# Twelve instead of eight weight pairs in the first pass of an MLP up-projection (Strassen-Winograd form, two-layer trunk)

## The chip, the cores and the metric

The kernel runs on one NeuronCore of a Trainium2 chip. The metric is the device time of one execution in microseconds. TensorE does the matrix products, VectorE (DVE) and ScalarE (ACT) prepare their operands and take their results, GpSimd (POOL) does small work and issues the stores of intermediate results, and SyncE (SP) issues the loads. Each of these engines works through its own list of instructions in order; the lists are written at build time by a scheduler that simulates the program, and semaphores tie them together.

## The reference

A trunk of two layers on a residual stream of 1024 tokens x 1024 features. Layer 0 mixes tokens with multi-head latent attention, layer 1 with a gated linear recurrence (HGRN2). Each is followed by a squared-ReLU MLP with 4096 inner features, and every sub-layer is wrapped in two RMS norms:

```python
def sq_relu_mlp(h, w1, w2):
    a = jax.nn.relu(h @ w1)
    return (a * a) @ w2
...
    h = h + rms_norm(m, norm_gains[layer, 1])        # m: the token mixer's output
    a = rms_norm(h, norm_gains[layer, 2])
    h = h + rms_norm(sq_relu_mlp(a, mlp_w1[layer], mlp_w2[layer]), norm_gains[layer, 3])
```

All inputs and the output are float32.

## The kernel before, in words

**Products.** Every float32 operand is split into a high part (fp32r, made by ACT) and a low part (the rest, made by DVE from the high part): `split`, lines 76 and 77. A product then takes three matmuls (`mm3`, lines 81 to 83): high x high, high x low, low x high. The second matmul of the three needs the moving operand's low part, the third the weights' low part.

**The stages.** Attention, its output projection with the first norm, MLP of layer 0, recurrence, MLP of layer 1. Each MLP has an up part (`mlp_up`, 1024 to 4096 features) and a down part (`mlp_down`). The change is in `mlp_up`.

**The up part.** It forms w1-transposed times activations by one level of the Strassen-Winograd scheme, with seven block products in place of eight. The activations are four blocks: B11 and B21 are the two feature halves of tokens 0 to 511, B12 (the tile `whole`, or in layer 1 `acc`) and B22 those of tokens 512 to 1023. Four sums of these blocks, T1 to T4, are made by DVE in steps of 128 x 1024 and split (`tsums12`, `tsums34`, lines 742 to 763). The 4096 inner features are taken in 16 *pairs* of 128-column blocks, p = 0 to 15. For each pair seven products of 12 matmuls of 512 columns are made: with B11, with B21 (on top of the first, in the same PSUM bank), with T2, T1, T3, B22 and T4.

**Two passes.** The products with B11 and B21 need tokens 0 to 511 alone. So for the first `EARLY` pairs they are made ahead, while the last tokens of the stage before are still on their way through the norms, and then the T sums; what they give (`sP1`, the product with B11, and `h11`, the first output block) is stored to DRAM and loaded again in the second pass (abridged):

```python
            for p in range(0, EARLY, 2):
                with tc.high_priority(offset=AHEAD[layer]):
                    for i in (p, p + 1):
                        w12[i] = w_parts(raw_early(i))
                        first[i], sP1 = first_two(i, w12[i][:, :, :4])
                        POOL.dma_start(psp[i * P:(i + 1) * P, :], sP1)
                    for i in (p, p + 1):
                        add_second(i, first[i], w12[i][:, :, 4:])
            tsums12()
...
            for p in range(NP):
                rA, rB = raw_half(p, 0), raw_half(p, 1)
                if p < EARLY:          # h11 and sP1 are loaded; w_parts(rB[:, :, P:])
                    others(p, rA, rB, ...)
                else:                  # first_two, w_parts of rA's half and of all of rB, add_second
                    ...
```

For an early pair the second pass is the five other products, 60 matmuls; for any other pair it is all seven, 84 matmuls. `others` (line 824) makes two weight sums for DVE to split: `s12` (lines 826, 827; for T2 and T1) and `s34` (lines 832, 833; for T3 and B22), adds the products up (lines 837, 844, 848, 851, 854), squares them on ACT (806, 807) and stores six results per pair (line 803).

**Buffers that matter here.** In the first pass `sP1` and `h11` go through two buffers `he`, which are free again when their stores have landed. The split weights `w` have five buffers. The raw weights have three buffers `raw` in the up part, of 512 KB each: a first-pass load (`raw_early`, line 785, one per pair) takes turns in two of them, a second-pass load (`raw_half`, line 791, two per pair) in all three. The first-pass products lie in two PSUM banks `mm`, the products with T2 in two banks `tr`.

**What sets the order.** The scheduler alone. The first pass has a priority of its own (`AHEAD`); the T sums and the second pass stand in program order behind it, and the scheduler merges them by its own estimate of when operands are ready.

Of the kernel before, what the change touches and what calls it, by code (L numbers as in the profile page):

```python
# [36 lines left out]
ROPE_BASE = 10000.0  # L37
LAG = (150, 100, 250)
AHEAD = (150, 150)
EARLY = 8  # L40
SCALE = (NOPE + ROPE) ** -0.5


# [15 lines left out]
def trunk(ctx, tc, x, x_t, positions, norm_gains, mla_w_in, mla_q_norm, mla_kv_norm, mla_w_uq, mla_w_ukv, mla_w_o,  # L59
# [9 lines left out]
    def new(p, shape, dt, tag, bufs=None):  # L69
        uid[0] += 1  # L70
        kw = {} if bufs is None else {"bufs": bufs}
        return p.tile(shape, dt, tag=tag, name=f"{tag}_{uid[0]}", **kw)
# [629 lines left out]
    hsp = new(dram, [7, NP * P, 512], F32, "hsp")  # L702
    psp = new(dram, [EARLY * P, 512], F32, "psp")

    def mlp_up(layer):
# [4 lines left out]
        with tc.tile_pool(name=f"up{layer}", bufs=1, side="left", reuse_waits="tile") as wp:  # L710
# [54 lines left out]
            def product(ps, w, X, more=False):  # L765

                for k in range(4):
                    mm3(ps, (w[:, 0, k], w[:, 1, k]), (X[:, 0, k], X[:, 1, k]), not more and k == 0, k == 3, more)
# [5 lines left out]
            def h512():  # L774
                tag = ring[hs["n"] % len(ring)]
                assert tag != "h2" or hs["more"]
                hs["n"] += 1
                p, bufs = {"he": (G, 2), "h": (wp, NH), "h2": (hs["more"], NM)}[tag]
                return new(p, [P, 512], F32, tag, bufs)
# [8 lines left out]
            def raw_half(p, kh):  # L788
                hs["r"] += 1
                r = new((wp, G0, G)[hs["r"] % 3], [P, 1024], F32, "raw").rearrange("p (k c) -> p k c", c=256)  # L790
                SP.dma_start(r, w1[:, kh * 4:(kh + 1) * 4, p * 256:(p + 1) * 256])
                return r
# [12 lines left out]
            def act2(h, src):  # L805
                ACT.activation(h, src, AF.Relu)
                ACT.activation(h, h, AF.Square)  # L807

            def first_two(p, wa):

                a = new(PG, [P, 512], F32, "mm")
                product(a, wa, B11)
                sP1 = h512() if p >= EARLY else new(G, [P, 512], F32, "he", 2)
                ACT.activation(sP1, a, AF.Copy)  # L814
                return a, sP1

            def add_second(p, a, w12):
                product(a, w12[:, :, :, :P], B21, True)
                h11 = h512() if p >= EARLY else new(G, [P, 512], F32, "he", 2)
                act2(h11, a)  # L820
# [50 lines left out]

            for p in range(0, EARLY, 2):

# [16 lines left out]
            for p in range(NP):  # L890
                rA, rB = raw_half(p, 0), raw_half(p, 1)
                if p < EARLY:
                    h11 = h512()
# [495 lines left out]
```

## Time and profile before

| | us |
|---|---|
| median of three runs | 2336.49 (2329.7 to 2338.51) |
| the profiled execution's own time | 2335.4 |
| its span, first to last instruction | 2333.7 |
| TensorE busy | 2266.3 (97%), 11487 matmuls |
| DVE busy | 1595.5 (68%) |
| ACT busy | 1170.1 (50%) |
| DMA | 333.12 MB, mean 143 GB/s |

The up part of layer 0 lies at about 480 to 806 us of the span, that of layer 1 at about 1693 to 2025 us. A matmul's record in this profile is longer than its step, because matmuls are pipelined: in a full stretch one of 512 columns starts every 0.227 us, while its record lasts 0.39 us. So a busy share near 100% is not a full TensorE; the count of matmuls in a stretch of fixed length, and the starts in the timeline, tell more. A stretch counts every instruction that touches it, those across its ends too.

### The profile page before, as it was taken

To read this page: it belongs to the slowest core of one execution; us is meant where nothing else is said; L and a number is where in the kernel's file an instruction comes from. 1 tells how busy PE (TensorE), PEld (TensorE's weight loads), DVE (VectorE), ACT (ScalarE), POOL (GpSimd) and SP (SyncE) were. 2 spreads that over 40 slices of the span, in tenths; PEclk is the share of its full clock that TensorE was granted. 3 is DMA by queue.
4 is the path that set the end of the run, shared out by engine and by line. 5 is a ranking of instruction groups with operands and counts; after the bars stand their busy time and mean duration, and the time that the engine had idled before them with its cause. 6 is when DMAs were issued, how large, how long until landed. Compare 5 with 4: busy or idle time off the path is not lost. (4 is left out here: it accounts for less than half of the span.)

```text
span 2333.7 us, 30701 instructions
## 1 busy us (share of the span) xinstructions
PE 2266.3 (97%) x11487; PEld 1912.8 (82%) x11487; DVE 1595.5 (68%) x2287; ACT 1170.1 (50%) x1893; POOL 346.1 (15%) x718
## 2 busy tenths in 40 slices
PE   8999999998999999999999999999989999999998
PEld 8789998876788888888888888888777888888886
DVE  5658886378766557588666667756678776566696
ACT  5436554364444444445565546755464444444443
POOL 1300000021222100001232213312121221100001
PEclk9999999999999999999999999999999999999999
DMA  7010002464654484565612334222355644663664
GB/s 221 23 33 10 10 10 71 145 231 161 219 171 162 167 288 144 180 215 177 207 47 90 101 98 136 79 76 73 95 186 191 222 155 149 222 238 114 223 214 158
DMA packets 229283, 333.12 MB, mean 143 GB/s; under 512 B 16743, under 2 KB 136590, under 8 KB 229134
## 3 DMA queue, kind: packets, MB, share of 16 engines
q1 hardware_dynamic: 205326, 251.45, 33.4%
q0 software_dynamic: 23808, 79.71, 9.3%
q8 instruction: 90, 1.47, 0.3%
q14 instruction: 59, 0.48, 0.1%
HBM read 247.22 MB, written 83.89 MB: 142 GB/s over the span
## 5 line engine op out<-in xcount | busy, mean ns | idle before, releaser
L77 DVE TENSOR_TENSOR w<-raw,w 128x1024 fp32r<-128x1024 f32 (+1 forms) x240 | 278.1, 1164 | 165.4 <-ACT w L76 164.6
L76 ACT ACTIVATE w<-raw 128x1024 fp32r<-128x1024 f32 (+1 forms) x240 | 237.8, 996 | 211.6 <-PE mm L83 82.4
L81 PE MATMUL mm<-A,w 128*128 128x512 f32 x832 | 329.6, 397 | 6.8 <-ACT he L814 2.9
L82 PE MATMUL mm<-A,w 128*128 128x512 f32 x832 | 327.4, 394 | 0.6 <-DVE A L77 0.6
L83 PE MATMUL mm<-A,w 128*128 128x512 f32 x832 | 325.7, 393 | 0.0
L76 ACT ACTIVATE w<-s 128x1024 fp32r<-128x1024 f32 x156 | 164.8, 1059 | 312.0 <-PE tr L83 120.5
L77 DVE TENSOR_TENSOR w<-s,w 128x1024 fp32r<-128x1024 f32 x156 | 190.2, 1221 | 140.8 <-ACT w L76 140.3
L81 PEld LDWEIGHTS mm<-A,w 128*128 128x128 f32 x832 | 157.5, 189 | 43.2 <-ACT he L814 4.0
L145 POOL TENSOR_TENSOR rstd<-rstd,nhalf 128x1 f32<-128x1 f32 x56 | 44.4, 794 | 965.5 <-DVE rstd L144 939.0
L83 PEld LDWEIGHTS mm<-A,w 128*128 128x128 f32 x832 | 157.3, 189 | 32.9
L82 PEld LDWEIGHTS mm<-A,w 128*128 128x128 f32 x832 | 157.4, 189 | 32.5 <-DVE A L77 1.0
L82 PE MATMUL mm<-w,w 128*128 128x512 f32 x432 | 168.6, 390 | 0.7 <-DVE w L77 0.7
L83 PE MATMUL mm<-w,w 128*128 128x512 f32 x432 | 168.3, 390 | 0.0
L81 PE MATMUL mm<-w,w 128*128 128x512 f32 x432 | 154.2, 391 | 0.8 <-DVE y L1036 0.4
L803 POOL DMA_DIRECT2D hsp<-h x176 | 94.8, 540 | 349.0 <-ACT h L807 176.8
L81 PE MATMUL mm<-w,A 128*128 128x256 f32 (+2 forms) x352 | 111.8, 320 | 4.3 <-ACT A L76 3.5
L83 PE MATMUL mm<-w,A 128*128 128x256 f32 (+2 forms) x352 | 111.3, 318 | 0.0
L82 PE MATMUL mm<-w,A 128*128 128x256 f32 (+2 forms) x352 | 110.6, 316 | 0.0
L83 PE MATMUL c<-T,w 128*128 128x512 f32 x256 | 99.4, 391 | 4.4 <-DVE w L77 4.4
L81 PE MATMUL c<-T,w 128*128 128x512 f32 x256 | 100.3, 392 | 1.6 <-ACT w L76 1.6
L82 PE MATMUL c<-T,w 128*128 128x512 f32 x256 | 99.7, 389 | 0.0
L81 PEld LDWEIGHTS mm<-w,w 128*128 128x128 f32 x432 | 81.0, 188 | 19.2 <-ACT u L1034 0.8
(441 smaller groups left out, 5648.4 us busy)
## 6 DMA issues: line engine op xcount, KB each, us to landing
raw<-in_mlp_w_dram SPq DMA_DIRECT2D x92, 512.0 KB, 5.0
hsp<-h POOLq DMA_DIRECT2D x176, 256.0 KB, 3.2
s<-in_mlp_w_dram SPq DMA_DIRECT2D x80, 512.0 KB, 5.9
raw<-hsp SPq DMA_DIRECT2D x76, 512.0 KB, 3.9
raw<-in_hgrn_w_in_dram SPq DMA_DIRECT2D x64, 512.0 KB, 4.2
sx<-hsp SPq DMA_DIRECT2D x36, 512.0 KB, 4.0
hsp<-he POOLq DMA_DIRECT2D x48, 256.0 KB, 3.3
xt<-in_x_dram SPq DMA_DIRECT2D x16, 512.0 KB, 6.1
```

Of the source, the lines that this page charges most:

```text
L76: ACT.activation(dst[:, 0], src, AF.Copy)
L77: DVE.tensor_tensor(dst[:, 1], src, dst[:, 0].bitcast(F32), ALU.subtract)
L81: PE.matmul(ps, lhs[0], rhs[0], start=start, stop=False, skip_group_check=more)
L82: PE.matmul(ps, lhs[0], rhs[1], start=False, stop=False, skip_group_check=more)
L83: PE.matmul(ps, lhs[1], rhs[0], start=False, stop=stop, skip_group_check=more)
L145: POOL.tensor_tensor(r, r, nhalf[:, :1], ALU.pow)
L803: POOL.dma_start(hsp[i, p * P:(p + 1) * P, :], h)
```

## The change

One constant grows: the first pass takes pairs 0 to 11, not 0 to 7. The scratch tensor `psp` follows it in size.

```diff
-EARLY = 8
+EARLY = 12
```

In each layer, pairs 8 to 11 thus get 24 matmuls ahead of the T sums' products instead of between their own other products. Each of them then has one load of 512 KB more (`raw_early`), one store more (`psp`, 256 KB) and two loads more (`h11` and `sP1`, 256 KB each). The matmuls are the same in number. The splits too are the same in their elements: in the first pass one of 1024 columns (the B11 and the B21 weights together), in the second one of 512 less by the first half and one of 512 instead of 1024.

How the scheduler's lists move is seen at three places, all in layer 0; layer 1 is alike but for details that the text names. In the names, `s` is a sum, `T_858`, `T_854`, `T_856`, `T_855` are T1, T2, T4 and T3, `whole` is B12, `A_748` to `A_750` are B11, B21 and B22; the last number of a name is a tile's own number.

**DVE, where the T sums begin.** Before:

```order
L745 TENSOR_TENSOR s_5376<-whole_4349,A_748_4343 128x1024
L77 TENSOR_TENSOR A_750_4345<-tr_5059,A_750_4345 128x4x128
L746 TENSOR_TENSOR s_5376<-s_5376,A_748_4343 128x1024
L747 TENSOR_TENSOR s_5377<-A_750_4345,s_5376 128x1024
L745 TENSOR_TENSOR s_5386<-whole_4349,A_748_4343 128x1024
L748 TENSOR_TENSOR s_5377<-s_5377,A_750_4345 128x1024
L77 TENSOR_TENSOR T_858_5079<-s_5376,T_858_5079 128x1024
L746 TENSOR_TENSOR s_5386<-s_5386,A_748_4343 128x1024
L77 TENSOR_TENSOR T_854_5075<-s_5377,T_854_5075 128x1024
L747 TENSOR_TENSOR s_5387<-A_750_4345,s_5386 128x1024
```

With the change:

```order
L745 TENSOR_TENSOR s_5524<-whole_4349,A_748_4343 128x1024
L77 TENSOR_TENSOR A_750_4345<-tr_5059,A_750_4345 128x4x128
L746 TENSOR_TENSOR s_5524<-s_5524,A_748_4343 128x1024
L747 TENSOR_TENSOR s_5525<-A_750_4345,s_5524 128x1024
L745 TENSOR_TENSOR s_5534<-whole_4349,A_748_4343 128x1024
L77 TENSOR_TENSOR T_858_5079<-s_5524,T_858_5079 128x1024
L748 TENSOR_TENSOR s_5525<-s_5525,A_750_4345 128x1024
L746 TENSOR_TENSOR s_5534<-s_5534,A_748_4343 128x1024
L77 TENSOR_TENSOR w_5399<-raw_5397,w_5399 128x1024
L77 TENSOR_TENSOR w_5452<-raw_5450,w_5452 128x1024
L747 TENSOR_TENSOR s_5535<-A_750_4345,s_5534 128x1024
```

The weight splits of pairs 9 and 10 (`w_5399`, `w_5452`) now stand among the T sums; that of pair 11 follows six rows later. From the row behind line 746's second to the end of pair 0's second weight split (`s34`) there are 27 rows with the change, 22 of them of 1024 columns and 5 of 512.

**DVE, where pair 1 begins its second pass.** Before, its sums (`s_5542`, `s_5548`) and the split of the first of them (`w_5545`) stand together:

```order
L77 TENSOR_TENSOR w_5453<-s_5435,w_5453 128x1024
L844 TENSOR_TENSOR h_5469<-mm_5456,h_5451 128x512
L826 TENSOR_TENSOR s_5542<-raw_5531,raw_5533 128x4x128
L77 TENSOR_TENSOR T_855_5076<-s_5426,T_855_5076 128x1024
L77 TENSOR_TENSOR w_5539<-raw_5533,w_5539 128x512
L832 TENSOR_TENSOR s_5548<-raw_5531 128x4x128
L827 TENSOR_TENSOR s_5542<-s_5542,raw_5531 128x4x128
L833 TENSOR_TENSOR s_5548<-raw_5533,s_5542 128x4x128
L848 TENSOR_TENSOR h_5484<-c_5471,h_5469 128x512
L77 TENSOR_TENSOR w_5545<-s_5542,w_5545 128x1024
```

With the change:

```order
L77 TENSOR_TENSOR T_855_5076<-s_5574,T_855_5076 128x1024
L77 TENSOR_TENSOR w_5601<-s_5583,w_5601 128x1024
L826 TENSOR_TENSOR s_5690<-raw_5679,raw_5681 128x4x128
L832 TENSOR_TENSOR s_5696<-raw_5679 128x4x128
L827 TENSOR_TENSOR s_5690<-s_5690,raw_5679 128x4x128
L833 TENSOR_TENSOR s_5696<-raw_5681,s_5690 128x4x128
L77 TENSOR_TENSOR w_5687<-raw_5681,w_5687 128x512
L826 TENSOR_TENSOR s_5803<-raw_5792,raw_5794 128x4x128
L832 TENSOR_TENSOR s_5809<-raw_5792 128x4x128
L827 TENSOR_TENSOR s_5803<-s_5803,raw_5792 128x4x128
L833 TENSOR_TENSOR s_5809<-raw_5794,s_5803 128x4x128
L77 TENSOR_TENSOR w_5693<-s_5690,w_5693 128x1024
```

The T sums are all done before pair 1 begins, and the four sums of pair 2 (`s_5803`, `s_5809`) now stand between pair 1's sums and the split `w_5693` of the first of them. In layer 1 the same four stand there.

**SP, the loads around the end of the first pass.** Before (line 785 is a first-pass load, 791 one half of a pair's second-pass weights, 894 and 896 the loads of `h11` and `sP1`):

```order
L785 DMA raw_5323<-in_mlp_w_dram 128x8x128
L791 DMA raw_5396<-in_mlp_w_dram 128x4x256
L791 DMA raw_5398<-in_mlp_w_dram 128x4x256
L791 DMA raw_5531<-in_mlp_w_dram 128x4x256
L894 DMA he_5400<-hsp_5068 128x512
L896 DMA he_5402<-psp_5069 128x512
L791 DMA raw_5533<-in_mlp_w_dram 128x4x256
```

With the change:

```order
L785 DMA raw_5450<-in_mlp_w_dram 128x8x128
L791 DMA raw_5679<-in_mlp_w_dram 128x4x256
L785 DMA raw_5471<-in_mlp_w_dram 128x8x128
L791 DMA raw_5544<-in_mlp_w_dram 128x4x256
L791 DMA raw_5546<-in_mlp_w_dram 128x4x256
L791 DMA raw_5681<-in_mlp_w_dram 128x4x256
L791 DMA raw_5792<-in_mlp_w_dram 128x4x256
L791 DMA raw_5794<-in_mlp_w_dram 128x4x256
L791 DMA raw_5905<-in_mlp_w_dram 128x4x256
L791 DMA raw_5907<-in_mlp_w_dram 128x4x256
L894 DMA he_5548<-hsp_5068 128x512
L896 DMA he_5550<-psp_5069 128x512
```

The weights of pairs 0 to 3 are now asked for ahead of pair 0's `h11` and `sP1`, where before three halves were. On TensorE, 60 matmuls (72 in layer 1) stand between the end of pair 7's first-pass products and the first matmul with T2, where before there were none; 76 stand ahead of the first that needs the low part of pair 0's first weight sum, 120 ahead of the first with T3, and 136 ahead of the first that needs the low part of pair 1's. The last three counts are the same in both layers. The lists of the recurrence between the two MLPs differ in places too, with the same instructions but for one load of an ACT function table fewer.

## The prediction, made before the changed kernel ran

> **What bounds the kernel now.** I read the page first, for the engine that is full; then the busy times by 100 us, for where that engine is not; then the same by 10 us, and the timelines of TensorE and DVE in the stretches found.
>
> ```profile
> span 2333.7 us, 30701 instructions
> PE 2266.3 (97%) x11487; PEld 1912.8 (82%) x11487; DVE 1595.5 (68%) x2287; ACT 1170.1 (50%) x1893; POOL 346.1 (15%) x718
> ...
> 500.00:600.00 100.00, 88.27 (x369) 69.88 (x368) 80.40 (x98) 48.72 (x73) 16.25 (x30) 0.95 0.52 177
> 600.00:700.00 100.00, 99.49 (x438) 81.64 (x437) 74.57 (x106) 47.49 (x69) 23.70 (x44) 1.00 0.59 195
> ...
> 1700.00:1800.00 100.00, 86.57 (x368) 68.96 (x367) 80.77 (x97) 50.23 (x77) 19.29 (x33) 0.95 0.52 173
> 1800.00:1900.00 100.00, 100.00 (x443) 82.81 (x442) 76.15 (x110) 46.51 (x68) 23.68 (x44) 1.00 0.63 213
> ```
>
> The columns of a stretch are its length, then busy time and instructions of TensorE, its weight loads, DVE, ACT and POOL, then the granted TensorE clock, the DMA share and GB/s. TensorE sets the time: a full 100 us hold 443 matmuls, one per 0.226 us. Two stretches hold 369 and 368, 149 matmuls or 34 us short together, and these lie where each MLP goes over from its first pass to its second. Nothing else the change touches has slack of this size.
>
> ```profile
> 533.40:560.80 27.40, 20.43 (x67) 15.09 (x67) 25.25 (x29) 13.02 (x17) 1.08 (x2) 0.81 0.37 122
> 1740.20:1766.10 25.90, 16.78 (x53) 12.38 (x53) 24.97 (x27) 9.88 (x11) 0.54 (x1) 0.80 0.33 108
> ...
> 533.17 0.39 PE L83 MATMUL mm<-A,w 128*128 128x512 f32 x1
> 535.19 0.50 PE L81 MATMUL tr<-T,w 128*128 128x512 f32 x1 [1.63 <-ACT w L76]
> 538.89 0.80 PE L83 MATMUL tr<-T,w 128*128 128x512 f32 x1 [2.49 <-DVE w L77]
> 541.19 0.63 PE L82 MATMUL tr<-T,w 128*128 128x512 f32 x1
> 541.62 0.63 PE L83 MATMUL tr<-T,w 128*128 128x512 f32 x1
> 549.78 0.50 PE L83 MATMUL c<-T,w 128*128 128x512 f32 x1 [2.18 <-DVE w L77]
> 560.58 0.39 PE L82 MATMUL c<-T,w 128*128 128x512 f32 x1
> 560.81 0.39 PE L83 MATMUL tr<-T,w 128*128 128x512 f32 x1
> ...
> 1740.01 0.39 PE L83 MATMUL mm<-A,w 128*128 128x512 f32 x1
> 1743.87 0.50 PE L81 MATMUL tr<-T,w 128*128 128x512 f32 x1 [3.48 <-ACT w L76]
> ```
>
> In layer 0 the first pass ends with the matmul at 533.17; the next could start at 533.40. TensorE then waits for splits of the weight sums of pair 0, which stand on DVE among the T sums, and DVE is busy 25.25 of 27.40 us. The matmul at 560.81 is the 67th of the stretch, so 66 are done before it. 66 x 0.227 us (the pace of starts in a full stretch, as from 560.58 to 560.81) = 15.0 us of work in 27.4: **12.4 us lost.** In layer 1, 52 matmuls (53 less the last) take 11.8 us of 25.9: **14.1 us lost.** A part of it is a lower clock: the starts 541.19 and 541.62 are 0.43 us apart.
>
> **The change part by part.** *Cover gained.* 96 matmuls per layer come ahead of this point, 21.8 us. What has to be ready, and when, follows from DVE's own steps:
>
> ```profile
> 525.06 1.22 DVE L746 TENSOR_TENSOR s<-s,A 128x1024 f32<-128x1024 f32 x1
> 526.20 1.22 DVE L77 TENSOR_TENSOR T<-s,T 128x1024 fp32r<-128x1024 f32 x1
> 544.43 0.68 DVE L832 TENSOR_TENSOR s<-raw 128x512 f32<-128x512 f32 x1
> 545.03 0.68 DVE L833 TENSOR_TENSOR s<-raw,s 128x512 f32<-128x512 f32 x1
> ...
> 1733.81 1.22 DVE L746 TENSOR_TENSOR s<-s,A 128x1024 f32<-128x1024 f32 x1
> ```
>
> A step of 1024 columns takes 1.135 us from start to start, one of 512 columns 0.60. Up to the second step of line 746, which ends at 526.2, the list has the same steps as before. Then come 27 to the end of pair 0's second weight split: 22 x 1.135 + 5 x 0.60 = 28.0, so 554.2. The raw weights of pair 0 may add 1.2 us: they wait for the slot of pair 11's first-pass weights, whose split ends 8 steps after 526.2, at 535.3, and a load takes 4.6 us:
>
> ```profile
> L791 SPq DMA_DIRECT2D raw<-in_mlp_w_dram x64: 367/368/577, 503.3 to 1967.1; - x64
> ...
>   DVE s L826: 32.2, 18
> ...
> DMA to landing us min/median/max: 3.7/4.6/8.5
> ```
>
> So all T sums and pair 0's weights are ready at 555.4. TensorE needs the last of them for T3, 120 matmuls after 533.4, at 560.6; the T2 product needs pair 0's first split 76 matmuls after, at 550.6, and that split is six steps from the end (four of 1024, two of 512), done at 549.7. In layer 0 nothing is late here. In layer 1 the same two are 1757.4 (1740.2 + 17.2) and 1758.3 (three and two steps before the 1762.9 of the next part): **0.9 us** of waiting. The four extra splits cost DVE nothing: pairs 8 to 11 have as many columns to split as before, and it lies under matmuls in both places. So the 12.4 and 14.1 us go: **26.5 us.**
>
> *What is late next.* DVE's list now has pair 2's four sums ahead of the split that pair 1's T2 product needs. They read raw weights, of which three buffers exist, and DVE waited for raw weights at line 826 eighteen times before, 32.2 us in all (row above). Step by step in layer 0: pair 0's buffer is read to the end by line 832, at 555.4 less 1.135 (the second split), 1.135 (the last T3 split) and 0.6 (line 833) = 552.5; pair 1's second half lands there 4.6 us later, 557.1; three sums of pair 1 free the third buffer at 558.9; pair 2's second half lands in it at 563.5; four sums, 565.9; then pair 1's split, **567.0**. TensorE needs it 136 matmuls after 533.4, at 564.2: **2.8 us** of waiting. Layer 1, the same from 1733.8 (here 28 steps follow a step earlier in the list, 23 x 1.135 + 5 x 0.60 = 29.1, with no wait for pair 0): 1762.9, buffer free at 1760.0, landed 1764.6, third buffer free 1766.4, landed 1771.0, split done **1774.5**, needed at 1740.2 + 0.9 + 30.8 = 1771.9: **2.6 us**, and 20 matmuls later **0.8 us** more, where line 844 of pair 0, which the B22 product waits for, stands behind pair 3's load (done 1779.8, needed 1779.0). Together 0.9 + 2.8 + 2.6 + 0.8 = **7.1 us back.** Bounds: with the shortest landing, 3.7 us, two loads in a row at each place save 1.8 us each, and 7.1 falls to 3.5; with the longest, 8.5 us, they add 7.8 us each, 15.6, and 7.1 grows to 22.7.
>
> *The clock.* A stall can cost more than itself.
>
> ```profile
> 540.00:542.00 2.00, 2.00 (x6) 1.56 (x5) 2.00 (x2) 0.00 (x0) 0.00 (x0) 0.50 0.23 84
> ...
> 589.18 0.47 PE L81 MATMUL tr<-T,w 128*128 128x512 f32 x1 [2.37 <-DVE h L837]
> 590.22 0.51 PE L83 MATMUL tr<-T,w 128*128 128x512 f32 x1 [0.34 <-DVE w L77]
> 590.56 0.40 PE L81 MATMUL tr<-T,w 128*128 128x512 f32 x1
> 590.80 0.40 PE L82 MATMUL tr<-T,w 128*128 128x512 f32 x1
> ...
> 1785.72 0.50 PE L81 MATMUL mm<-A,w 128*128 128x512 f32 x1 [1.27 <-DVE h L844]
> 1793.64 0.50 PE L83 MATMUL tr<-T,w 128*128 128x512 f32 x1 [1.26 <-DVE w L77]
> ```
>
> After two idle stretches of 1.63 and 2.49 us the clock was 0.50, and some 11 matmuls took 0.43 us instead of 0.227, 2.2 us. After a single one of 2.37 us (589.18) starts stayed 0.24 us apart. My 2.8 and 2.6 us are nearest that row, so I add nothing; the bound is 2.2 us per layer. [...]
>
> *DMA, SP, POOL.* The eight pairs bring 8 x 1.25 MB more, some 10 MB, 30 us of DMA time (177 GB/s at a share of 0.52 make 340 GB/s at a full one), spread over two up parts of 330 us whose share was 0.52 to 0.63. From 600 and from 1800 us on, early pairs already ran their second pass at 438 and 443 matmuls per 100 us, with all these loads and stores. So I cost them at nothing as long as the loads of `h11` and `sP1` keep off the raw weights (a rival below). In the first pass a buffer `he` holds one `sP1` and one `h11` for each two pairs:
>
> ```profile
> 499.00 0.60 ACT L806 ACTIVATE he<-mm 128x512 f32<-128x512 f32 x1 [2.70 <-DMA psp<-he]
> 504.19 0.50 PE L81 MATMUL mm<-A,w 128*128 128x512 f32 x1 [1.52 <-ACT he L814]
> ...
> DMA to landing us min/median/max: 2.3/2.7/5.9
> ...
> DMA to landing us min/median/max: 2.3/3.2/7.4
> ```
>
> The last two are the stores of `sP1` and of all results. With 0.6 us for the copy, 1.2 for the two steps of `h11` and 0.54 for each issue on POOL, a buffer turns round in 2.9 + 2.7 + 3.2 = 8.8 us, under the 10.9 us of two pairs' matmuls; a wait of 1.52 us at TensorE did come of it once. No cost, up to 1.5 us per layer.
>
> *Sum.* 26.5 - 7.1 = 19.4 us. Against the profiled execution's own 2335.4 us (1.7 more than its span) that gives 2316.0; the median of the runs is 1.1 us above that execution, so **2317 us**.
>
> **The rivals.** *The whole gap goes (2305).* If pair 1 is not late, and the waits at 589.18 and 590.22 (2.7 us) and the two of layer 1 (1.27 and 1.26) vanish as well, since DVE is no longer behind there, the gain is 26.5 + 5.2 = 31.7: 2336.5 - 31.7 = 2305. For it: DVE has 21.8 us more time before TensorE comes. Against it: the three raw buffers.
>
> *The stall only moves (2334).* Pairs 1 and 2 each wait 2.8 + 0.8 us and the clock halves for 2.2 more, in both layers: 4 x 5.8 + 0.9 = 24.1 of the 26.5 come back, 2336.5 - 2.4 = 2334. For it: in the list DVE reads pairs 2 and 3 ahead of what it owes TensorE. Against it: a pair's second pass is 13.6 us of matmuls, and two loads take 4.6 us each.
>
> *SP's list makes it slower (2358).* The four added pairs per layer load `h11` and `sP1` through the same in-order list as the raw weights.
>
> ```profile
> SPq L894 <- DMA hsp<-he: 27.2, 3, 16.0
> ```
>
> SP stood up to 16.0 us before such a load in layer 1. Where the wait exceeds what the raw buffers hold ahead, one pair's 13.6 us, the next raw load is late by a load's 4.6 us. Eight times that is 36.8 us, and a half clock after two of them 4.4: 2317 + 41 = 2358. Against it: the full rate from 600 and 1800 us on, where such pairs ran too.
>
> **How the numbers follow.** The forecast has 0.55 (its own range 2310, nothing back, to 2327, where half of the longer loads' 15.6 us and one half clock of 2.2 come on top), the full gap 0.15, the moved stall 0.19, the slower case 0.11. A run differs from another by up to 0.4% here, and 0.5%, 11.7 us, is about what a measurement can tell from no change. Faster by over 0.5%, below 2324.8, are the full gap and nearly all of the forecast: 0.67. Within it are the moved stall and the forecast's rest: 0.22. Slower 0.11. The range from 2303 to 2338 leaves out the slower case and the far ends, 2 in 10.
>
> **What would show it.** Right: the stretches 500 to 600 and 1700 to 1800 us hold over 420 matmuls each; the first T2 matmul has under 1 us of idle time before it; a wait of 2 to 3 us for DVE's `w` split (line 77) stands at TensorE some 31 us after the end of pair 7's first-pass products, and before it DVE waits for raw weights at line 826. Wrong: idle times on `w` or on lines 837 and 844 repeat at pairs 2 to 4; or DMA `raw` ends DVE's idle time at line 826 for far more than 32.2 us; or the first pass stalls on `he`.

## The result, and the profile after

The changed kernel takes **2318.12 us** (median of 4 runs, 2317.87 to 2319.2), the kernel before 2336.21 beside it. The ratio is 0.9934, 95% interval 0.9922 to 0.9947: faster by 0.5 to 0.8%. The forecast was 2317. The time is as forecast; part of the way to it is not, as the rows show.

The head of the page after, and the same four stretches as before:

```profile
span 2316.2 us, 30767 instructions
PE 2262.7 (98%) x11487; PEld 1914.5 (83%) x11487; DVE 1599.4 (69%) x2287; ACT 1167.6 (50%) x1892; POOL 346.4 (15%) x726
...
500.00:600.00 100.00, 93.64 (x409) 75.72 (x408) 78.09 (x91) 53.79 (x82) 19.55 (x36) 0.98 0.60 199
600.00:700.00 100.00, 100.00 (x443) 82.77 (x442) 80.03 (x117) 45.78 (x66) 23.26 (x43) 1.00 0.65 221
...
1700.00:1800.00 100.00, 95.66 (x420) 77.74 (x420) 79.28 (x94) 53.86 (x84) 20.16 (x37) 0.98 0.60 195
1800.00:1900.00 100.00, 98.86 (x437) 81.53 (x436) 78.16 (x115) 43.35 (x62) 23.08 (x43) 1.00 0.66 224
```

Where the passes meet, TensorE now does 409 and 420 matmuls, not 369 and 368; the full rate is 443. So 40 and 52 matmuls, 9.1 and 11.8 us, have come back, and about 8 and 5 us are still lost. The stretch from 600 us on is as full as it was (443 matmuls, before 438), at a DMA share of 0.65 instead of 0.59: there the added loads and stores cost nothing that shows. The stretch from 1800 us on holds 437 instead of 443.

What TensorE waits for, by the view of its waits (total, times, longest, in us). Before:

```profile
PE tr L83 <- DVE w L77: 6.8, 5, 2.6
PE tr L81 <- ACT w L76: 5.1, 2, 3.5
PE c L83 <- DVE w L77: 4.4, 2, 2.2
PE mm L81 <- ACT he L814: 2.9, 2, 1.5
```

After:

```profile
PE mm L81 <- ACT he L814: 5.5, 5, 2.0
...
PE mm L81 <- DVE h L844: 2.6, 1, 2.6
PE tr L81 <- ACT w L76: 2.3, 2, 1.1
...
PE mm L81 <- DVE he L844: 1.1, 1, 1.1
...
PE tr L83 <- DVE w L77: 0.8, 1, 0.8
```

The waits for split weights (`w`), which were the gap, fall from 16.3 us in these rows to 3.1. Waits for the buffers `he` and at line 844 take their place. In TensorE's timeline after:

```profile
532.91 0.50 PE L81 MATMUL mm<-A,w 128*128 128x512 f32 x1 [1.98 <-ACT he L814]
...
534.30 0.63 PE L83 MATMUL mm<-A,w 128*128 128x512 f32 x1
...
537.28 0.46 PE L81 MATMUL mm<-A,w 128*128 128x512 f32 x1
...
550.98 0.39 PE L81 MATMUL tr<-T,w 128*128 128x512 f32 x1
...
567.30 0.39 PE L81 MATMUL tr<-T,w 128*128 128x512 f32 x1
...
568.21 0.39 PE L83 MATMUL tr<-T,w 128*128 128x512 f32 x1
...
590.42 0.50 PE L81 MATMUL mm<-A,w 128*128 128x512 f32 x1 [1.15 <-DVE he L844]
...
1771.78 0.50 PE L81 MATMUL mm<-A,w 128*128 128x512 f32 x1 [2.63 <-DVE h L844]
```

The matmul at 550.98 is the first product with T2. It waits for nothing: the gap is gone. Pair 1's product, from 567.30 on, doesn't wait either, though I had placed the next wait at its first use of the weights' low part (line 83, here at 568.21). Instead there are two other stalls.

**A stall inside the first pass** (532.91). ACT and POOL just before it:

```profile
524.25 2.00 ACT L76 ACTIVATE T<-s 128x1024 fp32r<-128x1024 f32 x2
526.14 0.62 ACT L807 ACTIVATE he<-he 128x512 f32<-128x512 f32 x1
526.67 0.58 ACT L814 ACTIVATE he<-mm 128x512 f32<-128x512 f32 x1
532.26 0.60 ACT L814 ACTIVATE he<-mm 128x512 f32<-128x512 f32 x1 [5.01 <-DMA hsp<-he]
...
527.06 0.54 POOL L803 DMA_DIRECT2D hsp<-he  x1 [3.80 <-ACT he L807]
...
528.00:532.00 4.00, 2.93 (x13) 2.07 (x12) 4.00 (x5) 0.00 (x0) 0.13 (x1) 1.00 1.01 324
```

Two splits of T sums, 2.00 us, stand on ACT's list ahead of the squaring of an `h11` (line 807). Its store is issued 2 us late, at 527.06, the buffer is free 5.2 us later, and only then can ACT copy the next `sP1` (532.26), which TensorE waits for. The last row is the stretch in which that store ran: the DMA share was 1.01, with the raw loads that SP had issued from 526 us on. That these made the store slow is likely, but was not tried.

**A late `sP1` of pair 0** (590.42 and 1771.78). Line 837 adds it to the product with T2, line 844 stands behind that, and the product with B22 waits for line 844. DVE and ACT after, then SP's issues:

```profile
573.59 0.69 DVE L837 TENSOR_TENSOR h<-tr,he 128x512 f32<-128x512 f32 x1 [2.23 <-DMA he<-psp]
...
575.84 0.63 ACT L806 ACTIVATE h<-h 128x512 f32<-128x512 f32 x1 [9.40 <-DVE h L848]
...
582.40 0.69 DVE L826 TENSOR_TENSOR s<-raw,raw 128x512 f32<-128x512 f32 x1 [1.04 <-DMA raw<-in_mlp_w_dram]
...
589.67 0.69 DVE L844 TENSOR_TENSOR he<-mm,h 128x512 f32<-128x512 f32 x1
...
1767.23 0.69 DVE L826 TENSOR_TENSOR s<-raw,raw 128x512 f32<-128x512 f32 x1 [2.69 <-DMA raw<-in_mlp_w_dram]
1770.31 0.69 DVE L837 TENSOR_TENSOR h<-tr,he 128x512 f32<-128x512 f32 x1 [1.66 <-DMA he<-psp]
...
527.33 36.80 SPq L791 DMA_DIRECT2D raw<-in_mlp_w_dram  x7
...
570.01 0.34 SPq L896 DMA_DIRECT2D he<-psp  x1
```

The load of `sP1` is issued at 570.01, after seven raw loads and after the last store out of `he`; that store is what SP waited for last, 3.2 us in layer 0 and 1.9 in layer 1 by the view of its own waits. DVE had been ready for `sP1` 2.23 us before it came. In layer 1 TensorE's wait is for pair 0's own line 844; DVE's list had stood 2.69 us for raw weights there, and then 1.66 us for `sP1`. In layer 0 it is for pair 1's line 844 (589.67), some steps further on: ACT gets pair 0's sums at 575.84, and the split of a raw tile stands behind that on its list, so the buffer is free late, the next raw load lands at 582.40, and DVE has no idle time from there to 589.67.

**Where the 17.5 us of span went.** From each profile I took four lengths: to the first first-pass matmul of layer 0, from there to the last sum of its down part (line 1036), from there to the first first-pass matmul of layer 1 (the recurrence), and the rest (layer 1's MLP). The rows are of one profile each; e1 to e9 are explained below.

| profile | to layer 0's MLP | layer 0's MLP | recurrence | layer 1's MLP | span |
|---|---|---|---|---|---|
| before (8, 8) | 482.5 | 617.1 | 590.9 | 643.2 | 2333.7 |
| after (12, 12) | 482.8 | 606.4 | 594.0 | 633.1 | 2316.2 |
| e1 (12, 8) | 480.4 | 605.0 | 594.4 | 640.0 | 2319.8 |
| e2 (8, 12) | 481.3 | 617.8 | 593.0 | 632.9 | 2325.1 |
| e3 (10, 10) | 481.2 | 607.4 | 592.5 | 634.5 | 2315.6 |
| e4 (14, 14) | 481.3 | 612.3 | 599.1 | 631.5 | 2324.1 |
| e6 (12, 12) | 482.1 | 600.3 | 595.0 | 635.1 | 2312.4 |
| e7 (8, 8), less DVE work | 480.5 | 605.2 | 591.3 | 633.7 | 2310.7 |
| e9 (12, 12) | 480.8 | 598.1 | 593.5 | 627.6 | 2300.1 |

The MLPs gain 10.7 and 10.1 us. The recurrence between them, which the change doesn't touch, is 3.0 us longer.

### The profile page after: what moved, and what is told of

It reads as the page before. It is cut to its first block, busy times and chain, and to the rows that moved or that the text cites. A ratio compares the mean times of both kernels' runs of the same rounds, so it can differ in the third digit from the quotient of the medians.

```text
span 2316.2 us, 30767 instructions
## 1 busy us (share of the span) xinstructions
PE 2262.7 (98%) x11487; PEld 1914.5 (83%) x11487; DVE 1599.4 (69%) x2287; ACT 1167.6 (50%) x1892; POOL 346.4 (15%) x726
## 5 line engine op out<-in xcount | busy, mean ns | idle before, releaser
L806 ACT ACTIVATE h<-h 128x512 f32<-128x512 f32 x80 | 50.0, 626 | 93.7 <-DVE h L848 73.0
```

## The experiments

Times are medians, each with its ratio to the kernel before on the same chip, in brackets the 95% interval. By this measure the change itself is 0.9934 [0.9922, 0.9947]. All kernels here have a number of early pairs for each layer, as in e1's edit.

### One layer at a time (e1, e2)

```diff
-EARLY = 8
+EARLY = (12, 8)      # e1; e2: (8, 12)
-            for p in range(0, EARLY, 2):
+            for p in range(0, EARLY[layer], 2):
...
-                if p < EARLY:
+                if p < EARLY[layer]:
```

> Twelve pairs in the first pass of layer 0 alone, eight in layer 1. In the two traces, the start of the recurrence came 10.5 us earlier with the change and its end only 4.4 us earlier, and from there to the end of the program 13.1 us more were gained. Theory (the matmuls put ahead cover DVE's T sums; the recurrence loses some 6 us because the scheduler writes its lists differently once layer 0's are different): -10.5 + 6, so 2336.2 - 4.5 = 2331.7 us, and in the trace the recurrence is as long as with the whole change. Rival (the recurrence's loss has nothing to do with layer 0's lists): -10.5, so 2325.7 us. Rival (the T sums were not what TensorE waited for, the gain came from the loads asked for earlier): the stretch 500 to 600 us stays under 380 matmuls.

> Eight pairs in layer 0 and twelve in layer 1. Theory: layer 0 and the recurrence as before, layer 1 gains its 13.1 us: 2323.1 us. Rival (the recurrence's loss is not tied to layer 0): 2329 us. With the run of layer 0 alone the two gains should add up to the whole change's 18.1 us, -4.5 and -13.1 making -17.6.

Measured: e1 2323.05 us, 0.9954 [0.9937, 0.9972]; e2 2325.76 us, 0.9962 [0.9949, 0.9975]. Each layer carries a gap of its own: layer 0's MLP is 12.1 us shorter in e1, layer 1's 10.3 us in e2, and the other layer's moves by 0.7 and 3.1 us, less than the 8.8 us by which whole executions of the kernel before differ. The stretch from 500 to 600 us holds 413 matmuls in e1, so the rival with under 380 falls. The two gains add up to 0.84% against the 0.66% of the whole change, which the intervals allow. That layer 0 would bring much the lesser part was wrong, e1 lies nearer to its rival; e2 lies between the two. On the recurrence the pair of runs doesn't decide: it is 3.5 us longer in e1, whose lists there are new, and 2.1 in e2, whose lists are those of before. More profiles do, further below.

### How many pairs (e3, e4)

```diff
-EARLY = 8
+EARLY = (10, 10)     # e3; e4: (14, 14)
```

> Ten pairs in both layers. Theory (cover): two pairs more are 48 matmuls, 10.9 us, and bring two weight splits, 2.3 us, ahead of DVE's T sums; of 12.4 and 14.1 us lost, 12.4 - 10.9 + 2.3 = 3.8 and 5.5 stay, and the gain is 17.2 us less 0 to 6 us in the recurrence, so 2319 to 2325 us. Rival (the gain is proportional to the pairs moved): half of 18.1, so 2327 us.

> Fourteen pairs in both layers. Theory: with twelve no wait for the T products was left, so two pairs more cover nothing; 2318 us, give or take the 4 us that lists can differ by. Rival (proportional to the pairs moved): 18.1 x 6/4 = 27, so 2309 us. Rival (the added loads and stores, 2.6 MB per layer more again, begin to count on SP's list): slower than twelve by more than 4 us, above 2322 us.

Measured: e3 2317.52 us, 0.9931 [0.9914, 0.9948]; e4 2325.68 us, 0.9962 [0.9951, 0.9973]. Ten pairs are worth as much as twelve, a little more than my theory had (2319 to 2325): 48 matmuls of cover, 10.9 us, do nearly all of it. Both rivals that went by proportion (2327 and 2309) fall. Fourteen come out at the time of the rival by which the added loads count. By the table that is half of it: against after, 5.9 us more lie in layer 0's MLP and 5.1 us in the recurrence, and layer 1's MLP is 1.6 us shorter. TensorE and DVE of e4 show a late load in the MLP of layer 0 (the last row is a stretch of 5 us):

```profile
725.37 0.79 PE L81 MATMUL mm<-A,w 128*128 128x512 f32 x1 [4.00 <-DVE h L844]
...
723.90 0.69 DVE L837 TENSOR_TENSOR h<-tr,h 128x512 f32<-128x512 f32 x1 [4.78 <-DMA h<-psp]
...
725.00:730.00 5.00, 4.63 (x11) 3.67 (x12) 3.52 (x5) 2.21 (x3) 0.54 (x1) 0.50 0.15 55
```

An early pair's `sP1` comes late again, well inside the second pass, and a half clock (0.50, 11 matmuls in 5 us instead of 22) follows. Why e4's recurrence is the longest, 599.1 us, stays open.

### Is the gap DVE's list? (e7, e8)

Both leave out the four steps of the T sums that add low parts; e7 has eight pairs, e8 twelve.

```diff
-                    DVE.tensor_tensor(b, b, part(B11, 1, k), ALU.subtract)
...
-                    DVE.tensor_tensor(d, d, part(B22, 1, k), ALU.add)
...
-                    DVE.tensor_tensor(e, e, part(B21, 1, k), ALU.add)
...
-                    DVE.tensor_tensor(a, a, part(B22, 1, k), ALU.add)
```

> Eight pairs, and the four low-part steps of the T sums (lines 746, 748, 757, 762; eight steps per layer) are left out: the sums then use the high parts alone. DVE has 8 x 1.135 = 9.1 us less to do ahead of the T2 products in each layer. Theory (the gap is DVE's list being late, so either less list or more cover closes it): of the 12.4 and 14.1 us some 9 go in each layer, 2335.5 - 18 = 2317 to 2319. Rival (raw weights or ACT's splits hold the gap as well): half of it or less, 2326 or more.

> Twelve pairs with the same eight low-part steps left out in each layer. Theory (with twelve pairs the T sums are ready before TensorE asks, and what is late next waits for loads): nothing is won at the gap, 2318.1 less 0 to 3 us, 2315 to 2318. Rival (DVE's list still sets the time, only later): 9 us per layer more, 2300 to 2305.

Measured: e7 2316.23 us, 0.9915 [0.9898, 0.9931]; e8 2312.83 us, 0.9906 [0.9889, 0.9922]. With eight pairs, 9.1 us less of DVE work per layer are worth 0.85%, some 20 us: no less than the change, in the same place (layer 0's MLP 605.2 us, layer 1's 633.7). With twelve pairs the same work is worth 0.28%, 6.5 us by the ratios, and the intervals touch. So the gap was DVE's list being late, and cover and less list are two ways to the same end. The 6.5 us of e8 are more than the 0 to 3 of my theory and well under the rival's 9 per layer; as far as one profile tells, some 3 of them lie in layer 0's MLP, 603.5 us against 606.4. The longest wait left in e8 is for the late `sP1`, in layer 1, which has nothing to do with DVE's work: here DVE, with less to do, just waits longer for it.

```profile
1765.06 0.69 DVE L833 TENSOR_TENSOR h<-tr,he 128x512 f32<-128x512 f32 x1 [5.15 <-DMA he<-psp]
...
1766.54 0.50 PE L81 MATMUL mm<-A,w 128*128 128x512 f32 x1 [2.32 <-DVE h L840]
```

(Four lines are left out of e8's code, so its lines 833 and 840 are 837 and 844.)

### The late `sP1` (e6), and whether it matters without the change (e10)

```diff
-            ring = ["he"] * 2 + ["h"] * NH + ["h2"] * NM
+            ring = ["h"] * NH + ["he"] * 2 + ["h2"] * NM
```

> Twelve pairs in both layers; in the second pass the ring of 512-column buffers begins with `h`, not with `he`. So pair 0's h11 and sP1 need not wait for the last stores out of `he`, and their loads stand ahead of pair 0's raw weights in SP's list, not behind pair 1's. Theory (pair 0's sP1 comes late because its load stands behind raw loads): DVE's idle time at line 837 for DMA he (2.23 us at 573.59, 1.66 at 1770.31) goes, and with it TensorE's waits at line 844 (1.15 us in layer 0; 2.63 us in layer 1 with about 1.7 us of lower clock behind it): 5.5 us, 2312 to 2313. Rival (raw weights at line 826, 2.69 us of idle time at 1767.23, hold DVE anyway): the waits stay at another line and the time is within 1.5 us of 2318.

> Eight pairs in both layers as before the change, and only the ring begins with `h` as in e6. Theory (the gap at the T sums hides a late sP1 of pair 0, so the ring is worth something only behind the twelve pairs): the 1.27 us of line 844 in layer 1 go at most, 2334 to 2336, no difference that can be told. Rival (the ring is a gain of its own): as in e6 against the change, 6 to 8 us, 2327 to 2329.

Measured: e6 2311.76 us, 0.9897 [0.9882, 0.9913]; e10 2334.89 us, 0.9996 [0.9985, 1.0006]. Pair 0 now takes `h`, which is free, and its `sP1` is issued from 513.5 us on, not at 570.01. The group of these loads in e6 (names, count, shortest, median and longest issue in ns, first and last start):

```profile
L896 SPq DMA_DIRECT2D h<-psp x22: 319/408/617, 513.5 to 1903.3; - x22
```

In layer 0 no wait is left at TensorE in the second pass of e6: not that on line 844 at 590.42, nor those of 1.15 and 0.78 us for `w` at 597 and 599 us; its MLP is 6.1 us shorter than after's. In layer 1 the 2.63 us of line 844 are gone as well, but the MLP is not shorter in this profile (635.1 us against 633.1): the first pass waits 4.8 us for `he` there, against 1.7 in after, and a later line 844 1.49 us. In all e6 takes 8.6 us less than the change by the ratios, a little more than the theory's 5.5. The edit takes away both what held this load: its place behind the raw loads, and its wait for the last store out of `he`; which of them weighs more, it doesn't tell. e10 shows that the same line is worth nothing with eight pairs. There pair 0's `sP1` is not late to begin with: in the kernel before its load is issued at 538.5 us in layer 0, and DVE's line 837 of pair 0 doesn't wait for it in either layer. **The late `sP1` is one part of what took the gap's place; the stall on `he` is the other.**

### The stall on `he` (e5, e9)

```diff
-                sP1 = h512() if p >= EARLY else new(G, [P, 512], F32, "he", 2)
+                sP1 = (h512() if p >= EARLY else new(wp, [P, 512], F32, "h", NH) if p >= 8 else
+                       new(G, [P, 512], F32, "he", 2))      # e9: if 4 <= p < 10, and the ring of e6
```

> Twelve pairs in both layers, but the sP1 of pairs 8 to 11 is written to the free `h` buffers of the up pool, not to `he`. The changed kernel loses 1.98 us of idle time on `he` at 532.91 and, at a mean clock of 0.83 from 530 to 540, about 1.7 us more; layer 1 loses 1.01 and 0.65 us on `he`. Theory (DVE's list after the first pass runs by its own clock, so a TensorE that comes earlier meets the next late result): the `he` waits go, and 2 to 3 us come back as a wait for pair 1's `w` split at about 564 us, as the prediction had it: 2316 to 2318, at most 2 us better than 2318.1. Rival (the stalls are independent of each other): all 5.3 us are won, 2313. If `he` waits stay, the two buffers are not what makes them.

> Twelve pairs, pair 0 in `h` as in e6, and the sP1 of pairs 4 to 9 also in `h`, so that `he` holds their h11 alone. In e6 TensorE still waited for `he` in the first pass: 0.67, 1.73 and 0.82 us in layer 0, 1.01, 1.43, 1.56 and 0.77 us in layer 1, 8.0 us in all. Theory (those waits are two buffers turning round too slowly, of which e5 freed the wrong pairs): most of them go, 5 to 8 us under e6, 2304 to 2307. Rival (they come from the store itself: a later copy of sP1 waits for an h11 store that ACT's T splits delayed, and h11 still goes through `he`): they stay at sP1 or move to h11, 2309 to 2312.

Measured: e5 2316.23 us, 0.9922 [0.9907, 0.9937], not to be told from the change; e9 **2302.61 us, 0.9862 [0.9846, 0.9879]**. e5 freed the wrong pairs. Its stall is where it was, and it is one of the first eight pairs, not an added one:

```profile
530.63 0.50 PE L81 MATMUL mm<-A,w 128*128 128x512 f32 x1 [1.84 <-ACT he L815]
```

With pairs 4 to 9 in `h` the stall goes, and no other appears; what is left for `he` (1.46 and 1.38 us) was there before the change too (1.52 and 1.35). TensorE in e9, all waits over 0.5 us from 500 us to the end of layer 0's MLP and from 1690 to 1900 us; and the two stretches:

```profile
501.97 0.50 PE L81 MATMUL mm<-A,w 128*128 128x512 f32 x1 [1.46 <-ACT he L815]
...
1695.98 0.50 PE L81 MATMUL mm<-A,w 128*128 128x512 f32 x1 [1.38 <-ACT he L815]
...
500.00:600.00 100.00, 98.54 (x443) 81.41 (x442) 84.40 (x102) 56.68 (x85) 21.70 (x40) 1.00 0.63 211
...
1700.00:1800.00 100.00, 100.00 (x446) 82.77 (x445) 85.02 (x105) 52.69 (x77) 19.78 (x37) 1.00 0.65 212
```

443 and 446 matmuls where there were 369 and 368: the place where the passes meet is full. e9 is the fastest kernel here, 1.4% under the one before and, by the ratios, 0.7% under the change.

### Is it SP's list? (e11, e12)

e11 is e3 (ten pairs) with the ring of e6. e12 is e11 with one line more:

```diff
-                    SP.dma_start(sP1, psp[p * P:(p + 1) * P, :])
+                    POOL.dma_start(sP1, psp[p * P:(p + 1) * P, :])
```

> Ten pairs in both layers with the ring of e6. Ten pairs without it took 2317.5, of which one wait at line 844 in layer 0 is 2.94 us with a lower clock behind it. Theory (the same late sP1 there): that wait goes, and as DVE's order in the recurrence is the one that took 592.5 us and not 594 to 595, it comes out 1 to 3 us under e6: 2309 to 2311. Rival (with two pairs less of cover the T sums or pair 1's split are late once sP1 is not): 2314 to 2318.

> As e11 (ten pairs, pair 0 in `h`), but POOL issues the loads of sP1 (line 896) and SP only those of h11 and the raw weights. In e11 pair 3's sP1 was issued at 601.5 us behind four raw loads that SP had begun to issue at 579.5, DVE waited 6.00 us for it at line 837 and TensorE 4.93. Theory (SP's in-order list makes sP1 late: a load of sP1 waits there for a raw buffer it doesn't need): the 4.93 us wait and the 1.63 us at line 844 go, 2322.9 less 5 to 8: 2315 to 2318. Rival (POOL's list holds it as well, behind stores that wait for the pair before): as long a wait at line 837 or 844, with DVE's releaser again DMA psp, 2321 or more.

Measured: e11 2322.94 us, 0.9944 [0.9928, 0.9960], not faster than ten pairs without the ring (the intervals overlap); e12 2339.70 us, 1.0025 [1.0013, 1.0036], slower than before the change. I missed both. In e11 the longest wait is for neither the T sums nor pair 1's split but for another late `sP1`, in TensorE's, DVE's and SP's timelines:

```profile
608.47 0.77 PE L81 MATMUL tr<-T,w 128*128 128x512 f32 x1 [4.93 <-DVE h L837]
...
607.63 0.69 DVE L837 TENSOR_TENSOR h<-tr,h 128x512 f32<-128x512 f32 x1 [6.00 <-DMA h<-psp]
...
579.51 21.05 SPq L791 DMA_DIRECT2D raw<-in_mlp_w_dram  x4
...
601.54 0.81 SPq L896 DMA_DIRECT2D h<-psp  x2
```

The scheduler put four raw loads, which wait for buffers from 579.5 to 600.6, ahead of it. On POOL's list it is no better, since POOL's stores wait for the results of the pair before. In e12:

```profile
604.35 0.54 POOL L803 DMA_DIRECT2D hsp<-h  x1 [2.55 <-ACT h L807]
604.88 0.55 POOL L896 DMA_DIRECT2D h<-psp  x1
...
609.59 0.69 DVE L837 TENSOR_TENSOR h<-tr,h 128x512 f32<-128x512 f32 x1 [4.80 <-DMA h<-psp]
...
1791.76 0.76 PE L81 MATMUL tr<-T,w 128*128 128x512 f32 x1 [5.34 <-DVE h L837]
```

So in both runs the load of an early pair was as late as what waited ahead of it on its list (issued at 601.54 us behind the raw loads, at 604.88 behind a store); the rival of e12 holds. It doesn't show that SP's list alone made e11 slow, since moving the loads also moved POOL's stores.

## Why the prediction was right, and where it was not

**The gap goes: right.** The first product with T2 waits for nothing in either layer, the waits for `w` fall by 13 us in the rows above, and e7 shows the gap to be what I took it for, DVE's list being late. The MLPs gain 10.7 and 10.1 us against 9.6 (12.4 less 2.8) and 9.8 (14.1 less 4.3) in the sum.

**"What is late next", 7.1 us: the size about right by luck, the place wrong.** The step that failed is the one that had TensorE wait 2.8 and 2.6 us for pair 1's weight split. In none of the profiles with twelve pairs does TensorE wait over 0.14 us for it (e6, 1762.44). My times for DVE's list were good: split done at 567.0 by the sum, at 566.2 after. But TensorE's first matmul that needs it is at 568.21 and not at 564.2, held up by the stall on `he` and the clock behind it. Where that stall is gone, in e9, the split is done at 560.1 and TensorE comes for it at 562.46; the lists are others there, so whether my wait would have come with the change's own lists and no stall is not shown. In its place stand, by the rows of after, waits of 1.98, 1.15, 1.15 and 0.78 us in layer 0 and of 1.01, 0.65, 2.63 and 1.15 us in layer 1, 10.5 us. Against these, the waits of 2.37, 0.34, 1.27 and 1.26 us that the prediction quotes from before are gone, 5.2 us. The 0.8 us of line 844 behind pair 3's load was the right line and half the reason: of the 2.63 us there, DVE stood 1.66 for pair 0's own `sP1`, which I hadn't seen, and the other 1.0 us fits the raw load (2.69 us at 1767.23) ahead of it.

**`he` at nothing: wrong.** I had bounded a stall at 1.5 us per layer from a turnaround of 8.8 us, with the median landing of the stores and nothing ahead of line 807 on ACT. The row at 524.25 shows two T splits there, and the store took 5.2 us to free the buffer, not 3.2. TensorE's 1.98 us is over the bound. e9 shows what these waits and the late `sP1` are worth together: some 16 us.

**The clock at nothing: wrong by about 3 us.** From 533.94 to 537.28 us eight matmuls take 3.34 us, not 1.82: 1.5 us lost behind the single idle time of 1.98 us. Behind the 2.63 us in layer 1 there are at least 1.3 more:

```profile
1772.00:1776.00 4.00, 4.00 (x12) 3.12 (x12) 2.95 (x4) 1.27 (x2) 0.54 (x1) 0.63 0.19 50
```

12 matmuls instead of 17.6 in these 4 us. Both lie under the bound of 2.2 that I gave, but I took the row nearest in length (2.37 us with no drop), and these two waits went otherwise.

**DMA, SP's issue time and POOL at nothing: right for the bandwidth.** 443 matmuls from 600 us on at a share of 0.65; DVE's idle time for raw weights at line 826 fell to 24.6 us from 32.2. The third rival's mechanism, early pairs' loads on SP's in-order list, is real and was the first cost to come back, but it showed at one pair per layer and not at four. With fourteen pairs (4.00 us at 725.37) and in e11 (4.93) it showed again.

**What the sum lacked: the recurrence.** The scheduler writes all lists in one go, and with another number of early pairs in layer 0 it also orders DVE's steps in the recurrence otherwise, over 300 us later. Kernels whose DVE list there is that of before take 590.9 (before), 593.0 (e2), 591.3 (e7) and 590.6 us (e10); those with the list of twelve pairs 594.0 (after), 594.4 (e1), 595.0 (e5), 595.0 (e6), 593.6 (e8) and 593.5 us (e9). The list of ten pairs gives 592.5 (e3), 594.8 (e11) and 594.4 us (e12), that of fourteen 599.1 (e4). So about 3 us of the gain are given back there (means of 591.5 and 594.2), from one profile of each kernel; profiles with one and the same list differ by up to 2.4 us. That the order of DVE's steps is the cause is an inference from this grouping, and which of the moved steps costs the time was not tried.

So the forecast hit by 1 us since errors stood against each other: the MLPs gained about 1 us more than my 19.4, and the recurrence took 3 back. That the MLPs came so near is luck too: 10.5 us of waits and 3 us of clock came where I had 7.1, and 5.2 us of old waits went that I had left standing. Of the marks I had named, the first T2 product was as written; 500 to 600 and 1700 to 1800 us hold 409 and 420 matmuls, not over 420; the wait for pair 1's split is missing. Of the marks of "wrong", the stall of the first pass on `he` was there, and so were idle times on `w` at pair 3 (1.15 and 0.78 us).

## What to carry to other kernels

When a gap is covered by more work ahead of it, the cover is worth as much as the gap is long and no more (here ten pairs, 0.9931, were worth what twelve were, 0.9934), and the price is what the cover writes out and must fetch again. Look for the *first* of these fetches: whose buffer it reuses, and what stands ahead of it on the in-order list that issues it; here one line that gave pair 0 a free buffer was worth half as much as the whole change, and nothing without it. Look as well at the buffers through which the cover's results leave: a second line that relieved them was worth about as much again. Where one scheduler writes the lists of the whole program, compare the stages that the change doesn't touch as well.

## What the runs showed of the hardware

In these runs no one length of wait tells the cases in which TensorE's granted clock fell from those in which it did not. After single waits of 1.98 us (after, 532.91) and 2.63 us (after, 1771.78) it fell, to 0.50 from 534 to 537 us and to 0.63 from 1772 to 1776 us. After 2.37 us (before, 589.18) it was 1.00 from 589 to 593 us, and after 1.84 us (e5, 530.63) and 2.33 us (e1, 530.70) it was 1.00 as well. The stretches of the last two:

```profile
530.00:535.00 5.00, 4.37 (x19) 3.64 (x20) 3.44 (x3) 4.77 (x8) 1.08 (x2) 1.00 0.31 101
...
530.00:535.00 5.00, 4.30 (x19) 3.58 (x20) 3.56 (x4) 4.72 (x8) 1.08 (x2) 1.00 0.32 100
```

The 1.98 us of after and the 2.33 us of e1 are the same stall on `he`; the clock fell behind the shorter and not behind the longer. What made the difference, the runs don't tell. In after the starts were 0.43 us apart from 534.30 us on, 1.4 us after TensorE had begun again. A store out of `he` there freed its buffer 5.2 us after its issue (527.06 to 532.26), at a DMA share of 1.01 from 528 to 532 us, against a median landing of 3.6 us for these stores in the same profile.
